# Recurrence of an RWKV-7 layer: another order of the woven projections and another split of them between inverses and carries

## The chip, the cores and the metric

The kernel runs on one core of one Trainium2 chip. The metric is the device time of one execution in microseconds (us). Engines: PE (TensorE, matmul), with PEld for its weight loads; DVE (VectorE); ACT (ScalarE); POOL (GpSimd); SP, whose queue issues nearly all DMAs. Each engine works through its own instructions in the order in which they stand; semaphores make one engine wait for another.

## The reference, cut to what matters

One layer: 640 tokens (512 of a latent grid, 128 of a context) of width 1024 go through a norm, one wide projection, two branches (RWKV-7 recurrence in both directions, neighbourhood attention), gates, an output projection and a gated feed-forward network. Everything is float32.

```python
u_rw, u_na, gate_rw, gate_na = jnp.split(h @ p["w_in"], IN_SPLITS, axis=-1)
o_rw, s_new = _rwkv_branch(u_rw, s0, p["shift_mu"], ...)
...
merged = (jax.nn.sigmoid(gate_rw) * (o_rw @ p["w_o_rwkv"])
          + jax.nn.sigmoid(gate_na) * (o_na @ p["w_o_na"]))

def _rwkv_branch(u, s0, mu, ...):
    u = _centred_shift(u, mu)          # u + mu0 * (prev - u) + mu1 * (next - u)
    r, k, v, wd, ad, gd = jnp.split(u, RW_SPLITS, axis=-1)
    ...
def _wkv_step(s, inp):                 # 8 heads of 64, forward and backward
    sa = jnp.einsum("bhvk,bhk->bhv", s, a)
    s = s * w[:, :, None, :] + sa[..., None] * b[:, :, None, :] + v[..., None] * k[:, :, None, :]
    return s, jnp.einsum("bhvk,bhk->bhv", s, r)
```

## The kernel before

**Stages.** The eight heads of the recurrence are handled in four stages (ct = 0 to 3), two heads of 64 features in one tile of 128 partitions by 640 tokens. The tokens are cut into 20 lines of 64 (ten forward, ten backward). A stage has three parts:

- `main`: products of keys inside a line (L1118, into `Nt`).
- `inv`, the inverse of a triangular 64x64 matrix per line. A recursion over s = 1 to 30 runs on DVE alone (L1228, L1242/L1246, L1235); then DVE transposes the result (L1255, L1257), PE multiplies half blocks (L1266), ACT copies them (L1271), DVE copies other blocks (L1274), PE multiplies again (L1280), and ACT and DVE write `Rt` (L1285). Beside the recursion PE makes products whose results DVE masks (L1149, L1152).
- `carry`: eight steps along the lines, each a chain of three parts: PE L1314 and ACT L1317; PE L1341 and ACT L1347; PE L1354 and DVE L1366, whose result the next step's L1314 reads. L1326, L1332 and L1371 are further small matmuls of a step.

**What runs beside them.** During carry ct the next stage is prepared (`prep`, L592 to L689: small matmuls, ACT exponentials, DVE products), in portions that `beside` hands out by a budget of ACT and DVE time per entry. In the last step, `last()` emits what is left of it, makes sure that the next r and v are there, and emits four L1097 (`akr`) and two L1100 on DVE; the next stage's L1118 reads what L1097 writes. The end of the former stage (`out`, L1378 to L1413) runs beside the next inverse.

**The woven matmuls.** PE also has the wide input projection to do: units of 48 matmuls 128x128 on 320 tokens (L192), each for 128 output columns: l0 to l2, k0 to k3, r0 to r3, v0 to v3 for the recurrence, g0 to g15 for the gates; then the merges a0 to a7 and b0 to b7. The generator `stream` runs the units in the order of `PRM["order"]`. I call one such matmul a fill. A unit's weights are loaded two units ahead by SP and cast when the unit before it has run an eighth: ACT writes the high part `whi` (L170), DVE or POOL the rest `wlo` (L171), by the unit's letter in `PRM["wl"]` (d or p).

What follows a unit differs. k, r and v have ACT copies into `U` (L505, L510, L511) and the centred shift: ACT L516 and DVE L517 and L519, each twice, 128 and 512 tokens wide; the shift of a later k, r or v writes the tile that the stage then reads. A gate has an ACT tanh (L538) for each half and a store of it by SP. These followers are emitted a few fills later (`later`, `tick`); in a carry they are held back and take slots of `beside`.

**The plan.** How many fills stand where is written by hand. `weave` takes one entry of `PRM["plan"]` at each yield of a stage's part:

```python
for _ in (_ for g in ((0,), gen, (0,)) for _ in g):
    p = next(plan)
    for _ in range(p[0]):
        if not next(fill, False):
            break
    for o_, n in zip(others, p[1:]):
        if bud:
            if n:
                beside(o_, bud[n - 1])
```

The first number of an entry is the fills. `inv` has 37 entries: one before it, one after its start, thirty after s = 1 to 30, one after the two transposes have been emitted and before L1266 (entry 32), then four around L1266, L1280 and L1285. `carry` has 26: one before, three for each of eight steps, one behind. All of this stands in PE's queue in the order written; PE cannot pass an instruction that waits.

Some units must wait: k(c+1) until the preparation has read the last k, r(c+1) until the bonus of stage c is done, v(c+1) until inverse c is done. `need` runs the stream on when a unit must be finished.

Of the kernel before, what the change touches and what calls it, by code (L numbers as in the profile page):

```python
# [26 lines left out]
PRM = dict(
    order=("l0 l1 k0 r0 v0 l2 g0 g1 g2 k1 g3 r1 g4 g5 v1 g6 g7 k2 r2 g8 g9 v2 g10 g11 k3 r3 g12 g13 v3 g15 g14 a0 a1 a2 a3 a4 a5 a6 a7 "
     "b0 b1 b2 b4 b3 b5 b6 b7"),
    plan=(  # L30
        "22.0 0.0 2.0 4.0",
        ("0.0.0 2.0.0 2.0.1 10.0.0 2.0.0 2.0.1 2.0.1 2.0.1 2.0.1 2.0.1 10.0.0 2.0.0 2.0.0 10.0.0 2.0.0 2.0.0 "
         "2.0.0 10.0.0 2.0.0 2.0.0 2.0.0 2.0.0 2.0.0 2.0.0 2.0.0 2.0.0 2.0.0 2.0.0 2.0.0 2.0.0 5.0.0 24.0.0 "
         "20.0.0 10.0.0 8.0.0 8.0.0 0.0.0"),
        ("10.0 1.0 12.1 0.2 0.0 8.1 6.2 0.0 8.1 6.2 0.0 8.1 12.2 0.0 8.1 6.2 0.0 8.1 6.2 0.0 7.1 5.2 0.0 9.1 "
         "6.2 6.0"),
        "22.0 2.0 2.0 2.0",
        ("0.0.0 0.0.0 2.0.1 10.0.0 1.0.0 2.1.1 2.1.1 2.1.1 2.1.1 1.1.1 10.0.0 3.0.0 2.0.0 2.0.0 2.1.0 2.1.0 "
         "2.0.0 10.0.0 2.0.0 2.1.0 2.1.0 2.1.0 2.1.0 2.1.0 12.1.0 2.1.0 2.1.0 2.1.0 2.0.0 2.1.0 5.0.0 24.0.0 "
         "20.0.0 10.0.0 8.0.0 8.0.0 0.0.0"),  # L40
        ("10.0 0.0 8.1 6.2 0.0 8.1 6.2 0.0 8.1 6.2 0.0 8.1 6.2 0.0 8.1 6.2 0.0 7.1 6.2 0.0 8.1 6.2 0.0 8.1 "
         "6.2 6.0"),
        "22.0 2.0 0.0 5.0",
        ("0.0.0 10.0.0 2.0.1 10.0.0 2.0.0 2.1.1 2.1.1 2.1.2 2.1.1 2.1.0 10.0.0 2.0.0 2.0.0 2.0.0 2.1.0 2.1.0 "
         "2.0.0 10.0.0 2.0.0 2.1.0 2.1.0 3.1.0 4.1.0 2.1.0 2.1.0 2.1.0 2.1.0 4.1.0 2.1.0 2.0.0 5.0.0 24.0.0 "
         "18.0.0 8.0.0 9.0.0 8.0.0 0.0.0"),
        ("10.0 0.0 8.1 14.2 0.0 8.1 6.2 0.0 8.1 6.2 0.0 0.1 6.2 0.0 8.1 6.2 0.0 8.1 6.2 0.0 8.1 6.2 0.0 8.1 "
         "6.2 6.0"),
        "22.2 0.0 4.0 6.0",
        ("0.0.0 16.1.0 8.1.1 9.0.0 2.1.0 8.1.1 8.1.1 8.1.1 8.1.1 0.1.1 0.1.0 0.0.0 0.1.0 0.1.0 0.1.0 0.1.0 "  # L50
         "6.1.0 7.1.0 6.1.0 6.0.0 6.0.0 6.0.0 0.0.0 6.0.0 6.0.0 7.0.0 6.0.0 6.0.0 6.0.0 6.0.0 6.0.0 6.0.0 "
         "11.0.0 8.0.0 8.0.0 2.0.0 0.0.0"),
        ("10.0 0.0 8.1 6.2 0.0 8.1 4.2 0.0 8.1 6.2 0.0 8.1 6.2 0.0 8.1 6.2 0.0 8.1 6.2 0.0 8.1 6.2 0.0 8.1 "
         "14.2 6.0"),
        "2 0 6 6 6 4 4 5 2 0 5 1 1 0 0"),
    qp=((0, 0, 7, 6, 7), (2, 5, 4, 4, 3, 2, 5, 3, 1)), ada=2, pa=1, pd=0,
    lw=(0, 0, 0, 0, 0, 2, 2, 2, 2, 2, 2, 2, 2, 2, 2, 2),
# [1931 lines left out]
```

## Time and profile before

| | us |
|---|---|
| median of three runs | 1223.24 (1219.85 to 1223.52) |
| the profiled execution | 1220.16 |
| its span, first to last instruction | 1218.4 |
| recurrence in it: first L1118 to last matmul of carry 3 | 276.2 to 690.7 |
| first L1118 of stages 0 to 3 | 276.2, 376.2, 481.2, 587.8 |
| first L1266 of stages 0 to 3 | 316.1, 426.1, 528.9, 648.3 |
| first L1314 of stages 0 to 3 | 326.7, 436.5, 538.9, 655.4 |

In the rows of the profile, `fl<-h,whi` is a fill that reads `h` and `whi`; a number in brackets at the end of a timeline row is the idle time of that engine before it, and what ended it. Matmuls overlap, so the price of one is read from the distance of starts and not from its own length. The granted clock is a share of full speed.

### The profile page before, as it was taken

How to read it: one execution, taken by the hardware profiler on the slowest of the kernel's cores; microseconds unless marked ns; L12 is line 12 of the kernel's file. 1: busy time of each engine (PE TensorE's matmuls, PEld its weight loads, DVE VectorE, ACT ScalarE, POOL GpSimd, SP SyncE). 2: the span in 40 equal slices, each digit the busy share in tenths (PEclk: the TensorE clock that was granted, in tenths of full speed). 3: DMA queues.
4: the chain of work that ended last, by engine and by line, in shares of the span. 5: the costliest groups of instructions: out<-in, count | busy, mean ns of one | idle time of the engine just before them, and what ended most of it. 6: DMA issues, size and time to landing. Idle time of an engine off the chain costs nothing.

```text
span 1218.4 us, 26820 instructions
## 1 busy us (share of the span) xinstructions
PE 1141.9 (94%) x11160; PEld 1008.2 (83%) x11160; DVE 796.2 (65%) x1630; ACT 504.1 (41%) x1016; POOL 251.7 (21%) x273
## 2 busy tenths in 40 slices
...
GB/s 336 248 110 104 211 197 228 188 96 79 61 46 53 80 53 48 56 82 40 49 214 95 129 294 97 75 52 87 121 36 87 87 104 55 86 88 102 67 72 104
DMA packets 56577, 134.47 MB, mean 110 GB/s; under 512 B 7140, under 2 KB 22116, under 8 KB 56456
## 3 DMA queue, kind: packets, MB, share of 16 engines
...
q14 instruction: 33, 0.27, 0.1%
...
## 4 chain that ended last, share of the span: by engine, by line
PE 61%; DVE 15%; ACT 4%; issue 3%; DMA 2%; POOL 0%; SPq 0%; DVEq 0%; ACTq 0%; POOLq 0%
PE f L1708 20%; PE acc L279 16%; PE fl L192 10%; DVE pr L1242 2%; DVE RL L1246 2%; PE mm L192 2%; PE w L1314 1%; PE w L1354 1%; PE w L1341 1%; PE w L1326 1%; DVE RL L1235 1%; PE po L939 1%; DVE AG L1149 1%; DMA wst<-in_w_o_dram 1%; DVE wlo L171 1%
## 5 line engine op out<-in xcount | busy, mean ns | idle before, releaser
L192 PE MATMUL fl<-h,whi 128*128 128x320 f32 x704 | 173.6, 328 | 1.8 <-ACT U L505 0.9
L1708 PE MATMUL f<-t,whi 128*128 128x320 f32 x640 | 142.4, 311 | 0.0
L1708 PE MATMUL f<-b,whi 128*128 128x320 f32 x608 | 135.6, 310 | 2.1 <-ACT b L181 1.8
L279 PE MATMUL acc<-whi,u 128*128 128x512 f32 (+1 forms) x448 | 136.0, 385 | 0.0
L192 PEld LDWEIGHTS fl<-h,whi 128*128 128x128 f32 x704 | 123.7, 196 | 6.7 <-ACT U L505 1.2
L171 POOL TENSOR_TENSOR wlo<-wst,whi 128x1024 fp32r<-128x1024 f32 (+2 forms) x37 | 79.7, 2153 | 207.0 <-ACT whi L170 203.6
L192 PE MATMUL fl<-h,wlo 128*128 128x320 f32 x352 | 116.3, 330 | 1.4 <-POOL wlo L171 1.4
L170 ACT CAST whi<-wst 128x1024 fp32r<-128x1024 f32 (+2 forms) x86 | 81.8, 957 | 76.8 <-PE acc L279 30.4
L1708 PEld LDWEIGHTS f<-t,whi 128*128 128x128 f32 x640 | 108.0, 189 | 0.0
L1708 PEld LDWEIGHTS f<-b,whi 128*128 128x128 f32 x608 | 101.9, 188 | 3.3 <-ACT b L181 2.2
L1708 PE MATMUL f<-t,wlo 128*128 128x320 f32 x320 | 99.4, 311 | 0.0
L1763 POOL TENSOR_TENSOR ws<-wst 128x512 f32<-128x512 f32 x20 | 27.6, 1381 | 341.2 <-DVE wlo L1752 226.7
L279 PEld LDWEIGHTS acc<-whi,u 128*128 128x128 f32 x448 | 83.5, 188 | 16.6
L1708 PE MATMUL f<-b,wlo 128*128 128x320 f32 x304 | 94.3, 310 | 2.2 <-DVE wlo L1752 2.2
L1749 ACT CAST whi<-ws 128x1024 fp32r<-128x1024 f32 x40 | 42.0, 1051 | 108.6 <-PE f L1708 47.5
L279 PE MATMUL acc<-wlo,u 128*128 128x512 f32 (+1 forms) x224 | 86.3, 385 | 0.0
L171 DVE TENSOR_TENSOR wlo<-wst,whi 128x1024 fp32r<-128x1024 f32 (+1 forms) x49 | 60.1, 1234 | 35.7 <-ACT whi L170 34.9
L279 PE MATMUL acc<-whi,h 128*128 128x512 f32 x240 | 79.2, 404 | 0.3 <-DVE h L393 0.3
L192 PEld LDWEIGHTS fl<-h,wlo 128*128 128x128 f32 x352 | 69.1, 196 | 4.2 <-POOL wlo L171 1.7
L192 PE MATMUL mm<-h,whi 128*128 128x320 f32 x288 | 69.5, 327 | 2.5 <-ACT U L505 2.5
L1548 DVE SCALAR_TENSOR_TENSOR tt<-acc,G 128x512 f32<-128x512 f32 (+1 forms) x51 | 34.7, 681 | 50.6 <-PE acc L279 50.6
L192 PE MATMUL fl<-o,whi 128*128 128x320 f32 x224 | 57.2, 335 | 6.6 <-DMA o<-o_d 5.2
...
## 6 DMA issues: line engine op xcount, KB each, us to landing
...
```

Source lines behind the costliest of these rows:

```text
L170: act.copy(hi[:, :n], st[:, :n])
L171: (eng or dve).tensor_tensor(out=lo[:, :n], in0=st[:, :n], in1=hi[:, :n].bitcast(F32), op=ALU.subtract)
L192: pe.matmul(ps[:, :t1 - t0], w[:, a:a + 128], x[:, k0 + kt, t0:t1], start=n == 0, stop=n == 3 * nk - 1)
L279: pe.matmul(pss[i][:, a:b], lhs(x, kt, ts_), w[:, cs_], start=ki == 0 and n == 0, stop=ki == last and n == 2)
L939: pe.matmul(pso[64 * hd:64 * hd + 64, :128], vt[:, hc:hc + 64], blk[k][hd][:, c * 128:(c + 1) * 128], start=c == 0, stop=c == len(vts) - 1)
L1149: dve.tensor_tensor(out=AG[oth, ls, h, :], in0=sq(pg, n)[oth], in1=V(K[oth, :], [[0, n], [1, 64]], KO["strict"]), op=ALU.mult)
L1242: dve.tensor_tensor(out=prv, in0=V(RL[:, s + 1 + a, :], [[32, b - a], [0, s]], s), in1=V(RL[:, s, :], [[0, b - a], [1, s]]), op=ALU.mult)
L1246: dve.tensor_tensor(out=dst, in0=dst, in1=prv, op=ALU.add)
L1548: dve.scalar_tensor_tensor(out=tt, in0=ps[:, a:b], scalar=c, in1=G[:, g, sl], op0=ALU.mult, op1=ALU.mult)
L1708: pe.matmul(ps[:, :H2], w_[:, c_], x_[:, kt, :], start=first and kt + n == 0, stop=last and kt == 3 and n == 2, skip_group_check=more)
L1749: act.copy(r[0][:, :width], src())
L1763: eng_x(PRM["se"][i - 1]).tensor_tensor(out=o_, in0=x, in1=y, op=op)
```

## The change

Only numbers and letters of `PRM` change. No instruction of PE is added or removed, and the fills sum to 1364 before and after.

- **Plan.** In stages 0 to 2, the entries of s = 18 to 27 (in stages 1 and 2 of s = 18 to 26) get two fills more, and the entry after s = 30 gets 38 for 24. Most entries of the carries get two fills less, a few four.

| fills of the plan | inverse 0 | carry 0 | inverse 1 | carry 1 | inverse 2 | carry 2 | inverse 3 | carry 3 |
|---|---|---|---|---|---|---|---|---|
| before | 165 | 132 | 164 | 127 | 167 | 128 | 188 | 134 |
| after | 199 | 98 | 196 | 95 | 199 | 96 | 188 | 134 |

- **Order.** r1, r2, r3 move behind two or three gates, and k2 and k3 move ahead of one. Followed through the plan, this is where units and what follows them come to stand:

| | before | after |
|---|---|---|
| inverse 0, s = 18 to its end | r1, g4 | g4, g5, most of r1 |
| shift of r1 | after the transposes of inverse 0 | carry 0, steps 0 and 1 |
| shift of v1 | carry 0, step 6 | carry 0, step 5 |
| inverse 1 | g7, k2, r2, g8 | k2, g7, g8, g9, part of r2 |
| shift of r2 | after the transposes of inverse 1 | carry 1, step 2 |
| inverse 2 | g11, k3, r3, g12 | k3, g11, g12, g13, start of r3 |
| shift of r3 | after the transposes of inverse 2 | carry 2, steps 2 and 3 |
| v3 fills forced by `need` before stage 3 | 12 | 8 |

- **Casts.** `wlo` of k1, v1, g6, r2, v2, g10, v3 and g15 is made by DVE and not by POOL, that of a4 by POOL and not by DVE.

```diff
-    order=("l0 l1 k0 r0 v0 l2 g0 g1 g2 k1 g3 r1 g4 g5 v1 g6 g7 k2 r2 g8 g9 v2 g10 g11 k3 r3 g12 g13 v3 g15 g14 a0 a1 a2 a3 a4 a5 a6 a7 "
+    order=("l0 l1 k0 r0 v0 l2 g0 g1 g2 k1 g3 g4 g5 r1 v1 g6 k2 g7 g8 g9 r2 v2 g10 k3 g11 g12 g13 r3 v3 g15 g14 a0 a1 a2 a3 a4 a5 a6 a7 "
...
         "22.0 0.0 2.0 4.0",
-        ("0.0.0 2.0.0 2.0.1 10.0.0 2.0.0 2.0.1 2.0.1 2.0.1 2.0.1 2.0.1 10.0.0 2.0.0 2.0.0 10.0.0 2.0.0 2.0.0 "
-         "2.0.0 10.0.0 2.0.0 2.0.0 2.0.0 2.0.0 2.0.0 2.0.0 2.0.0 2.0.0 2.0.0 2.0.0 2.0.0 2.0.0 5.0.0 24.0.0 "
-         "20.0.0 10.0.0 8.0.0 8.0.0 0.0.0"),
-        ("10.0 1.0 12.1 0.2 0.0 8.1 6.2 0.0 8.1 6.2 0.0 8.1 12.2 0.0 8.1 6.2 0.0 8.1 6.2 0.0 7.1 5.2 0.0 9.1 "
-         "6.2 6.0"),
+        ("0.0.0 2.0.0 2.0.1 10.0.0 2.0.0 2.0.1 2.0.1 2.0.1 2.0.1 2.0.1 10.0.0 2.0.0 2.0.0 10.0.0 2.0.0 "
+         "2.0.0 2.0.0 10.0.0 2.0.0 4.0.0 4.0.0 4.0.0 4.0.0 4.0.0 4.0.0 4.0.0 4.0.0 4.0.0 4.0.0 2.0.0 "
+         "5.0.0 38.0.0 20.0.0 10.0.0 8.0.0 8.0.0 0.0.0"),
+        ("10.0 1.0 8.1 0.2 0.0 6.1 4.2 0.0 6.1 4.2 0.0 6.1 8.2 0.0 6.1 4.2 0.0 6.1 4.2 0.0 5.1 3.2 0.0 "
+         "7.1 4.2 6.0"),
...
-         "2.0.0 10.0.0 2.0.0 2.1.0 2.1.0 2.1.0 2.1.0 2.1.0 12.1.0 2.1.0 2.1.0 2.1.0 2.0.0 2.1.0 5.0.0 24.0.0 "
...
+         "2.1.0 2.0.0 10.0.0 2.0.0 4.1.0 4.1.0 4.1.0 4.1.0 4.1.0 14.1.0 4.1.0 4.1.0 4.1.0 2.0.0 2.1.0 "
+         "5.0.0 38.0.0 20.0.0 10.0.0 8.0.0 8.0.0 0.0.0"),
...
-    wl="dddddddddppppppppppppppppppppppppppdpppppppppppp", nu=9, na=(
+    wl="ddddddddddppppddppppdddpppppddppppppppppppppppp", nu=9, na=(
```

Stage 3's entries are the same, only wrapped differently.

More of the change, by code (lines that the diff above doesn't have):

```diff
@@ L31 @@
         "22.0 0.0 2.0 4.0",
-        ("0.0.0 2.0.0 2.0.1 10.0.0 2.0.0 2.0.1 2.0.1 2.0.1 2.0.1 2.0.1 10.0.0 2.0.0 2.0.0 10.0.0 2.0.0 2.0.0 "
-         "2.0.0 10.0.0 2.0.0 2.0.0 2.0.0 2.0.0 2.0.0 2.0.0 2.0.0 2.0.0 2.0.0 2.0.0 2.0.0 2.0.0 5.0.0 24.0.0 "
-         "20.0.0 10.0.0 8.0.0 8.0.0 0.0.0"),
-        ("10.0 1.0 12.1 0.2 0.0 8.1 6.2 0.0 8.1 6.2 0.0 8.1 12.2 0.0 8.1 6.2 0.0 8.1 6.2 0.0 7.1 5.2 0.0 9.1 "
-         "6.2 6.0"),
-        "22.0 2.0 2.0 2.0",
-        ("0.0.0 0.0.0 2.0.1 10.0.0 1.0.0 2.1.1 2.1.1 2.1.1 2.1.1 1.1.1 10.0.0 3.0.0 2.0.0 2.0.0 2.1.0 2.1.0 "
-         "2.0.0 10.0.0 2.0.0 2.1.0 2.1.0 2.1.0 2.1.0 2.1.0 12.1.0 2.1.0 2.1.0 2.1.0 2.0.0 2.1.0 5.0.0 24.0.0 "
-         "20.0.0 10.0.0 8.0.0 8.0.0 0.0.0"),
@@ L41 @@
-        ("10.0 0.0 8.1 6.2 0.0 8.1 6.2 0.0 8.1 6.2 0.0 8.1 6.2 0.0 8.1 6.2 0.0 7.1 6.2 0.0 8.1 6.2 0.0 8.1 "
-         "6.2 6.0"),
-        "22.0 2.0 0.0 5.0",
[L44 to L48, printed above, removed]
@@ L49 @@
-        "22.2 0.0 4.0 6.0",
[L50 to L54, printed above, removed]
+        ("0.0.0 2.0.0 2.0.1 10.0.0 2.0.0 2.0.1 2.0.1 2.0.1 2.0.1 2.0.1 10.0.0 2.0.0 2.0.0 10.0.0 2.0.0 "
+         "2.0.0 2.0.0 10.0.0 2.0.0 4.0.0 4.0.0 4.0.0 4.0.0 4.0.0 4.0.0 4.0.0 4.0.0 4.0.0 4.0.0 2.0.0 "
+         "5.0.0 38.0.0 20.0.0 10.0.0 8.0.0 8.0.0 0.0.0"),
```

16 lines of the change are left out of this document (added).

## The prediction

> **What bounds the kernel now.** I read the page's head first, for the engine that is busy and the engine that ends the chain.
>
> ```profile
> span 1218.4 us, 26820 instructions
> PE 1141.9 (94%) x11160; PEld 1008.2 (83%) x11160; DVE 796.2 (65%) x1630; ACT 504.1 (41%) x1016; POOL 251.7 (21%) x273
> PE 61%; DVE 15%; ACT 4%; issue 3%; DMA 2%; POOL 0%; SPq 0%; DVEq 0%; ACTq 0%; POOLq 0%
> ```
>
> TensorE is busy 94%, but the share is an average. So I cut the recurrence by stage: from the first half-product of an inverse (L1266) to the first carry matmul (L1314), which I call the tail, and from there to the next stage's L1118 (in stage 3 to the last carry matmul), which I call the carry. Columns: length, busy time and instructions of PE, PEld, DVE, ACT, POOL, then the granted clock.
>
> ```profile
> core 0: us, PE busy (x) PEld busy (x) DVE busy (x) ACT busy (x) POOL busy (x), PEclk, DMA share, GB/s
> 316.11:326.73 10.62, 10.62 (x196) 9.94 (x197) 7.25 (x15) 3.79 (x9) 0.48 (x1) 0.69 0.07 24
> 326.73:376.15 49.42, 47.63 (x624) 41.93 (x623) 25.21 (x41) 26.82 (x71) 10.81 (x11) 0.97 0.17 55
> 426.10:436.47 10.37, 10.37 (x197) 9.83 (x197) 7.36 (x15) 3.36 (x8) 1.32 (x2) 0.71 0.11 40
> 436.47:481.18 44.71, 44.70 (x619) 39.81 (x618) 22.65 (x38) 25.78 (x70) 12.35 (x12) 1.00 0.16 51
> 528.92:538.94 10.02, 10.02 (x195) 9.48 (x195) 9.18 (x13) 5.47 (x12) 4.48 (x4) 0.73 0.23 69
> 538.94:587.84 48.90, 48.09 (x637) 42.49 (x636) 23.21 (x42) 26.86 (x73) 10.28 (x11) 1.00 0.18 57
> 648.25:655.41 7.16, 7.16 (x189) 6.64 (x189) 6.63 (x14) 2.40 (x6) 0.82 (x1) 1.00 0.28 78
> ```
>
> In the carries of stages 0 to 2 PE works almost without a gap (47.63 of 49.42, 44.70 of 44.71, 48.09 of 48.90), with DVE and ACT about half busy. The tails are PE-busy too, but at 0.69 to 0.73 of the clock; stage 3's runs at 1.00. The waits of PE tell why; the rows are the ends of the inverses of stages 1, 2 and 3, a wait for weights in stage 1, and one wait in carry 0.
>
> ```profile
> PE w L1266 <- DVE f L1255: 2.6, 1, 2.6
> PE fl L192 <- POOL wlo L171: 1.4, 1, 1.4
> ...
> PE w L1266 <- DVE f L1255: 3.7, 1, 3.7
> ...
> PE w L1266 <- DVE f L1255: 0.2, 1, 0.2
> ...
> PE w L1314 <- DVE ZV L1366: 1.5, 1, 1.5
> ```
>
> The timeline has stage 0's wait, and the price of a woven matmul ("fill") before and after it:
>
> ```profile
> 309.02 0.46 PE L192 MATMUL fl<-h,whi 128*128 128x320 f32 x2
> ...
> 309.46 0.46 PE L192 MATMUL fl<-h,whi 128*128 128x320 f32 x2
> ...
> 316.11 1.48 PE L1266 MATMUL w<-f,Nt 32*32 32x32 f32 x80 [4.87 <-DVE f L1255]
> ...
> 318.75 0.73 PE L192 MATMUL fl<-h,whi 128*128 128x320 f32 x2
> ...
> 319.55 0.73 PE L192 MATMUL fl<-h,whi 128*128 128x320 f32 x2
> ```
>
> Three fills go by in 0.44 us (0.147 each) before the wait, in 0.80 (0.267) after it. So DVE bounds an inverse's end, PE idles there 4.9, 2.6 and 3.7 us and restarts at half clock, and PE bounds the carry.
>
> **Term 1, carries.** The plan's sums fall from 132, 127, 128 fills to 98, 95, 96 in stages 0 to 2: 98 fewer, 98 x 0.147 = 14.4 us less PE work. Does the chain behind them allow it? A step without other work, from stage 3:
>
> ```profile
> 676.08 0.54 ACT L1347 COPY ZV<-w 64x128 f32<-64x128 f32 x2 [0.55 <-PE w L1341]
> ...
> 677.33 0.45 PE L1354 MATMUL w<-ZV,TG 128*64 128x64 f32 x8
> ...
> 677.83 0.61 DVE L1366 TENSOR_TENSOR ZV<-w,Dt 64x128 f32<-64x128 f32 x2 [0.25 <-PE w L1354]
> ...
> 679.02 0.45 PE L1314 MATMUL w<-ZV,AG 128*64 128x64 f32 x8
> ```
>
> ACT is done at 676.62 and PE comes 0.71 later; DVE at 678.44, PE 0.58 later. Two fills fewer at each place (0.29) still leave PE last. Four things give time back.
>
> (a) Twelve of the 98 stand behind a carry's last L1366. There DVE leads: it runs on from L1366 to the four L1097 that L1118 needs.
>
> ```profile
> 365.81 0.61 DVE L1366 TENSOR_TENSOR ZV<-w,Dt 64x128 f32<-64x128 f32 x2
> 366.45 2.22 DVE L680 TENSOR_TENSOR f<-NK,pre 128x640 f32<-128x640 f32 x1
> ...
> 371.48 0.82 DVE L680 TENSOR_TENSOR f<-NK,pre 128x640 f32<-128x640 f32 x1
> ...
> 372.94 3.37 DVE L1097 TENSOR_TENSOR AG<-kk,P 64x640 f32<-64x640 f32 x4
> ```
>
> That ends at 376.31, and L1118 starts at 376.15. 12 x 0.147 = 1.8 us gain nothing.
>
> (b) r1, r2 and r3 were projected by an inverse's end; their shifts (four DVE operations, ACT copies ahead of them) ran in the tails. Now they fall into carry steps between L1347 and L1366. The row of v1's shift is the price: two of its operations
>
> ```profile
> 364.25 0.75 DVE L517 SCALAR_TENSOR_TENSOR vp<-U,C,vp 128x512 f32<-128x512 f32 x1
> 365.03 0.75 DVE L519 SCALAR_TENSOR_TENSOR vp<-U,C,vp 128x512 f32<-128x512 f32 x1
> ```
>
> held L1366 until 365.81 and PE for 1.5 us. What is late is the next step's L1314, and all PE work queued behind it. Bounds 0 (the shift lies under PE work) and 2.1 (1.5 and the four fills taken out of that step) each; I take 1.5: 4.5 us.
>
> (c) After that wait the clock fell:
>
> ```profile
> 366.15:368.00 1.85, 1.85 (x25) 1.41 (x25) 1.82 (x2) 0.62 (x2) 1.84 (x1) 0.77 0.00 0
> 368.00:370.00 2.00, 2.00 (x8) 2.00 (x9) 1.50 (x3) 1.24 (x3) 0.00 (x0) 0.50 0.51 133
> 370.00:372.00 2.00, 2.00 (x18) 1.60 (x17) 2.00 (x3) 1.40 (x4) 0.00 (x0) 0.85 0.44 173
> ```
>
> 0.23 x 1.85 + 0.50 x 2 + 0.15 x 2 = 1.7 us of PE lost. Three new waits could cost 0 to 5.2; stage 1's wait of 2.6 lowered the clock as well, so I take one of three, as they are shorter: 1.7. [...]
>
> (d) Shifts take slots from the preparation of the next stage: two of its 0.82 us operations come to stand behind the last L1366 in stages 0 and 1, one fewer in stage 2. In stage 0 POOL's cast, which stretched L680 to 2.22, comes earlier (-1.4). 1.6 - 1.4 + 1.6 - 0.8 = 1.0.
>
> Carries: -14.4 + 1.8 + 4.5 + 1.7 + 1.0 = -5.4 (from -14.4 to -0.1, with 6.3 and 5.2 for b and c).
>
> **Term 2, inverses up to L1266.** They get 34, 32 and 32 fills: 5.0, 4.7, 4.7 us. Against idle of 4.87 stage 0 ends 0.1 later. Stage 1 has 2.6, and the 1.4 and more that its fills waited for weights and U tiles: about even. In stage 2 PE alone would come 4.7 - 3.7 = 1.0 late. But DVE's own chain moves as well, by the casts, since gates now follow each other faster there:
>
> ```profile
> 312.86 1.16 DVE L1235 SCALAR_TENSOR_TENSOR RL<-RL 128x28 f32<-128x28 f32 x6
> ...
> 418.76 2.40 POOL L171 TENSOR_TENSOR wlo<-wst,whi 128x1024 fp32r<-128x1024 f32 x1
> ...
> 418.87 5.25 DVE L1235 SCALAR_TENSOR_TENSOR RL<-RL 128x28 f32<-128x28 f32 x6
> ...
> 512.52 1.89 DVE L1242 TENSOR_TENSOR pr<-RL 128x114 f32<-128x114 f32 x2
> ```
>
> The six L1235 take 1.16 us alone and 5.25 under two POOL casts: 2.0 each. In stage 2 a cast that POOL had to wait for costs 1.89 less some 0.46, 1.4. Stage 1 loses the two behind L1235 (-4.1), gets g9's earlier (+1.4 to 2.0) and r2's on DVE itself (+1.2):
>
> ```profile
> L171 DVE TENSOR_TENSOR wlo<-wst,whi 128x1024 fp32r<-128x1024 f32 (+1 forms) x49 | 60.1, 1234 | 35.7 <-ACT whi L170 34.9
> ```
>
> -1.2. Stage 2 gets g13's and r3's ahead of the transposes, 2 x 1.4 to 2 x 2.0: 3.5. Stage 0 keeps two. Sum: 0.1 - 1.2 + 3.5 = +2.4, between -1.2 (r3's cast falls beside the transposes, and PE is on time) and +5.
> [...]
> The other casts given to DVE (k1, v1, g6, v2, g10, v3, g15) lie where DVE is half busy; cover gone, 1.2 each.
>
> **Term 3, tails.** Stage 3's tail holds 28 fills in 7.16 us at full clock; stage 0's and 1's 36, stage 2's 35. At full clock: 7.16 + 8 x 0.147 = 8.34, 8.34, 8.19, that is -2.3, -2.0, -1.8 if PE does not idle at L1266. I take stage 0 whole, stage 1 half (DVE and PE arrive within 1 to 2 us), stage 2 nothing (DVE late by 2.5). -3.3; bounds -6.1 and 0.
>
> **Term 4, the rest.** Four of v3's matmuls fewer are forced before stage 3 (8 for 12) and come out behind the last carry: +0.6. a4's half-size cast goes from DVE to POOL in stage 3's inverse: half of 1.2 saved, at most half of 2.0 blocked, taken as 0. A gate issues two stores on SP that wait for its tanh, with the load for the unit after next behind them; one unit of 48 fills (7 us) covers that load, so 0.
>
> Sum: -5.4 + 2.4 - 3.3 + 0.6 = -5.7 on the profiled execution's 1220.16 us. The median of the runs is 1223.24, 3.1 above it; I carry the difference over: 1217.5.
>
> **Rivals.** *PE bounds everything.* Nothing stalls: -14.4, tails -6.1, inverses +1.1, +0.6: -18.8, 1204.4. For it: PE 44.70 of 44.71 in carry 1. Against: the row of v1's shift. Chance 0.14.
> *The vector engine's ring.* From L1366 through preparation, L1097 and the recursion to L1255 DVE does the same work wherever fills stand, and sets the carries too: their gain is 0; -3.3 + 2.4 + 0.6 = -0.3, 1222.9. For it: 365.81 to 376.31 without a gap. Against: DVE 22.65 busy of 44.71. Chance 0.21.
> *Slower: the clock.* With fewer fills in a carry every wait of 1.5 us there buys a half-clock window of 1.7. Two more in each of three carries: +10.2 - 5.7 = +4.5, 1227.7. It decides from the fourth further window on (3 x 1.7 = 5.1). For it: the 0.50 row. Against: carries 1 and 2 at 1.00 now. Chance 0.27.
>
> **How the numbers follow.** The forecast has 0.38, with its own range 1212 to 1220. 0.3% is 3.7 us, about what a measurement of this kernel can tell. Faster: 0.38 + 0.14 = 0.52; within: 0.21; slower: 0.27. The range, 1206 to 1229, leaves out most of the first rival and a clock that falls oftener than eight times in all.
>
> **What would show it.** Right: L1266 without a wait and the clock at 1.00 behind it in stage 0; clean carry steps of 3.7 us in place of 4.3 (679.02 less 0.59); L1314 waiting for L1366 where r's shift lies; L1235 short in stage 1 and long in stage 2. Wrong: carries of unchanged length with DVE busy throughout, or 0.50 in the middle of carries.

## The result, and the profile after

The changed kernel takes 1230.36 us (median of four runs, 1228.76 to 1231.55) where the kernel before took 1222.78 in the same comparison: a ratio of 1.0064, 95% interval 1.005 to 1.0078. It is slower by some 7.6 us; 1217.5 had been forecast. A second comparison gave 1.0052 (1.0027 to 1.0077).

The head of the page of after:

```profile
PE 1145.4 (93%) x11160; PEld 1008.4 (82%) x11160; DVE 802.9 (65%) x1637; ACT 504.1 (41%) x1016; POOL 226.7 (18%) x266
...
PE 65%; DVE 13%; ACT 4%; issue 2%; DMA 1%; SPq 0%; POOL 0%; DVEq 0%; ACTq 0%; POOLq 0%
```

It hardly differs from before's, and so does not tell where the time went. The cut by stage does. The rows are after's tails of stages 0 to 2, its carries 0 to 2, and its inverses of stages 2 and 3 up to L1266 (columns as in the prediction):

```profile
316.49:324.81 8.32, 8.32 (x197) 7.80 (x197) 6.40 (x12) 3.28 (x9) 1.00 (x2) 1.00 0.26 85
424.94:433.27 8.33, 8.33 (x197) 7.80 (x197) 6.71 (x12) 4.41 (x9) 1.32 (x2) 1.00 0.36 120
535.21:543.39 8.18, 8.18 (x195) 7.66 (x195) 6.17 (x12) 4.19 (x9) 0.13 (x1) 1.00 0.20 75
...
324.81:373.73 48.92, 43.72 (x590) 37.89 (x589) 26.94 (x46) 26.64 (x72) 5.18 (x10) 0.93 0.11 36
433.27:479.91 46.64, 42.21 (x588) 36.62 (x587) 25.77 (x43) 25.47 (x71) 7.85 (x12) 0.96 0.13 42
543.39:591.90 48.51, 45.63 (x600) 39.80 (x600) 25.64 (x45) 27.51 (x75) 7.00 (x10) 0.93 0.12 36
...
479.91:535.21 55.30, 47.43 (x848) 42.84 (x849) 48.40 (x141) 20.54 (x41) 15.41 (x15) 0.94 0.19 64
591.90:657.05 65.15, 50.52 (x843) 43.59 (x844) 44.49 (x148) 15.64 (x32) 15.38 (x15) 0.92 0.40 134
```

The same two inverses before:

```profile
481.18:528.92 47.74, 40.46 (x818) 36.74 (x817) 42.77 (x141) 18.89 (x38) 14.65 (x16) 0.99 0.17 60
587.84:648.25 60.41, 48.54 (x844) 43.78 (x844) 42.50 (x147) 17.26 (x35) 13.24 (x15) 0.92 0.43 145
```

The tails came down to 8.32, 8.33 and 8.18 at full clock: 6.2 us gained. The carries, with 98 fills fewer, changed by -0.5, +1.9 and -0.4: PE was idle there 2.6 us in all before (lengths less PE busy) and 12.5 after, and the clock stands at 0.93 to 0.96. The inverses grew by 0.3, 1.3, 7.6 and 4.7. Together: -6.2 + 1.0 + 13.9, and 1.6 behind the last carry: 10.3 of the 10.4 us between the two spans (1228.8 and 1218.4).

*Carry 0.* The timeline has DVE and POOL of after around its longest wait, the waits view what PE paid:

```profile
354.91 0.74 DVE L517 SCALAR_TENSOR_TENSOR vp<-U,C,vp 128x512 f32<-128x512 f32 x1
355.69 2.91 DVE L519 SCALAR_TENSOR_TENSOR vp<-U,C,vp 128x512 f32<-128x512 f32 x1
358.63 0.61 DVE L1366 TENSOR_TENSOR ZV<-w,Dt 64x128 f32<-64x128 f32 x2
...
355.71 2.34 POOL L171 TENSOR_TENSOR wlo<-wst,whi 128x1024 fp32r<-128x1024 f32 x1 [16.50 <-ACT whi L170]
```

```profile
PE w L1314 <- DVE ZV L1366: 4.0, 1, 4.0
```

L519 took 0.75 before. Now a cast of POOL starts 0.02 us behind it and L519 takes 2.91; L1366 stands behind it, and PE waits 4.0. The 2.16 us more are nearly the cast's whole 2.34, and over the 1.4 that I had mixed in. By the rows DVE starts first, by 0.02 us, and is the one that is held.

*Inverse 2.* The groups of DVE in that stretch, before and then after (columns: count | busy us, mean ns | idle):

```profile
L1242 DVE TENSOR_TENSOR pr<-RL 128x110 f32<-128x110 f32 (+22 forms) x48 | 11.7, 283 | 0.0
L1246 DVE TENSOR_TENSOR RL<-RL,pr 128x110 f32<-128x110 f32 (+22 forms) x48 | 10.7, 263 | 0.0
...
L1235 DVE SCALAR_TENSOR_TENSOR RL<-RL 128x28 f32<-128x28 f32 (+2 forms) x6 | 1.1, 238 | 0.0
```

```profile
L1246 DVE TENSOR_TENSOR RL<-RL,pr 128x110 f32<-128x110 f32 (+22 forms) x48 | 12.9, 308 | 0.0
L1242 DVE TENSOR_TENSOR pr<-RL 128x110 f32<-128x110 f32 (+22 forms) x48 | 12.4, 297 | 0.0
...
L1235 DVE SCALAR_TENSOR_TENSOR RL<-RL 128x28 f32<-128x28 f32 (+2 forms) x6 | 3.2, 596 | 0.0
```

As many instructions, and 2.2, 0.7 and 2.1 us more. The timeline of after shows why: two casts of POOL (g13's and r3's) and the two operations of DVE that they stretch.

```profile
526.43 2.41 POOL L171 TENSOR_TENSOR wlo<-wst,whi 128x1024 fp32r<-128x1024 f32 x1 [0.44 <-ACT whi L170]
530.74 2.41 POOL L171 TENSOR_TENSOR wlo<-wst,whi 128x1024 fp32r<-128x1024 f32 x1 [1.89 <-ACT whi L170]
...
526.33 2.62 DVE L1246 TENSOR_TENSOR RL<-RL,pr 128x75 f32<-128x75 f32 x2
...
529.91 3.29 DVE L1235 SCALAR_TENSOR_TENSOR RL<-RL 128x28 f32<-128x28 f32 x6
```

*Inverse 3.* The loads of `o` (L1426) overwrite the buffers of `h`, so they wait for the last fill of g14 (SP's L1426 for L192: 8.1 us before, 5.9 after). These fills in the inverse, with first and last start; before, then after:

```profile
L192 PE MATMUL fl<-h,wlo x18: 307/309/552, 592.2 to 606.8; 128*128 128x320 f32 x18
```

```profile
L192 PE MATMUL fl<-h,wlo x20: 302/309/415, 596.2 to 612.1; 128*128 128x320 f32 x20
```

SP's timeline has the loads; before, then after:

```profile
606.69 7.10 SPq L1426 DMA_DIRECT2D o<-o_d  x12
```

```profile
612.29 7.35 SPq L1426 DMA_DIRECT2D o<-o_d  x12
```

And the windows show the 8 us in which PE restarts on them; before, then after:

```profile
612.00:616.00 4.00, 3.48 (x13) 3.18 (x14) 0.13 (x1) 0.00 (x0) 0.00 (x0) 0.50 1.02 399
616.00:620.00 4.00, 3.99 (x28) 3.14 (x30) 4.00 (x16) 0.92 (x1) 0.00 (x0) 0.96 1.00 387
```

```profile
616.00:620.00 4.00, 3.05 (x11) 2.30 (x11) 1.51 (x6) 0.92 (x1) 0.00 (x0) 0.57 0.99 333
620.00:624.00 4.00, 3.66 (x9) 2.17 (x8) 0.00 (x0) 0.00 (x0) 0.00 (x0) 0.50 1.03 404
```

The load goes out 20.4 us behind the stage's start instead of 18.9. PE's first fill that reads `o` is no later for that (24.4 us behind the stage's start, 24.7 before). But half clock lasts through the second 4 us as well (0.50 for 0.96), with L1071 and L1086 of the inverse in PE's queue between those fills.

### The profile page after: what moved, and what is told of

Read it like the earlier page. It is cut to its first block, busy times and chain, and to the rows that moved or that the text cites. A ratio compares the mean times of both kernels' runs of the same rounds, so it can differ in the third digit from the quotient of the medians.

```text
span 1228.8 us, 26813 instructions
## 1 busy us (share of the span) xinstructions
PE 1145.4 (93%) x11160; PEld 1008.4 (82%) x11160; DVE 802.9 (65%) x1637; ACT 504.1 (41%) x1016; POOL 226.7 (18%) x266
## 4 chain that ended last, share of the span: by engine, by line
PE 65%; DVE 13%; ACT 4%; issue 2%; DMA 1%; SPq 0%; POOL 0%; DVEq 0%; ACTq 0%; POOLq 0%
PE f L1708 21%; PE acc L279 16%; PE fl L192 12%; PE mm L192 2%; DVE RL L1246 2%; DVE pr L1242 2%; PE w L1314 1%; PE w L1354 1%; PE w L1326 1%; PE w L1341 1%; DVE AG L1097 1%; PE po L939 1%; ACT L L905 1%; PE w L1140 1%; PE w L1332 1%
## 5 line engine op out<-in xcount | busy, mean ns | idle before, releaser
L192 PE MATMUL fl<-h,whi 128*128 128x320 f32 x704 | 171.1, 324 | 3.7 <-ACT fl L538 3.7
L192 PEld LDWEIGHTS fl<-h,whi 128*128 128x128 f32 x704 | 120.1, 191 | 9.1 <-ACT fl L538 4.2
L192 PE MATMUL fl<-h,wlo 128*128 128x320 f32 x352 | 113.3, 322 | 0.0
L171 DVE TENSOR_TENSOR wlo<-wst,whi 128x1024 fp32r<-128x1024 f32 x56 | 69.3, 1243 | 38.3 <-ACT whi L170 37.3
L171 POOL TENSOR_TENSOR wlo<-wst,whi 128x1024 fp32r<-128x1024 f32 (+2 forms) x30 | 56.3, 1878 | 161.5 <-ACT whi L170 161.5
L192 PE MATMUL mm<-h,whi 128*128 128x320 f32 x288 | 69.7, 327 | 2.2 <-ACT U L505 2.2
L192 PEld LDWEIGHTS fl<-h,wlo 128*128 128x128 f32 x352 | 67.1, 191 | 2.5 <-issue 0.2
L192 PE MATMUL fl<-o,whi 128*128 128x320 f32 x224 | 57.2, 335 | 9.6 <-DMA o<-o_d 4.8
```

The costliest lines, as they stand in the source:

```text
L171: (eng or dve).tensor_tensor(out=lo[:, :n], in0=st[:, :n], in1=hi[:, :n].bitcast(F32), op=ALU.subtract)
L192: pe.matmul(ps[:, :t1 - t0], w[:, a:a + 128], x[:, k0 + kt, t0:t1], start=n == 0, stop=n == 3 * nk - 1)
```

## The experiments

All lengths in us, from one profiled execution each: inverse from a stage's first L1118 to its first L1266, tail to its first L1314, carry to the next stage's L1118 (carry 3 is 35.3 to its last matmul in all of them). Times are medians, ratios against the runs of before beside them. Those had medians of 1222.78 (after), 1219.84 (e1 to e4), 1221.32 (e5 to e8), 1219.47 (e9, e10) and 1222.40 (e11), so kernels of different groups are compared by their ratios.

| kernel | inverses 0 to 3 | tails 0 to 3 | carries 0 to 2 | time | ratio, 95% |
|---|---|---|---|---|---|
| before | 39.9 50.0 47.7 60.4 | 10.6 10.4 10.0 7.2 | 49.4 44.7 48.9 | 1222.78 | |
| after | 40.2 51.2 55.3 65.2 | 8.3 8.3 8.2 7.2 | 48.9 46.6 48.5 | 1230.36 | 1.0064 (1.005 to 1.0078) |
| e1_plan | 42.1 52.6 56.2 64.9 | 9.8 9.4 10.4 9.2 | 47.8 44.5 43.7 | 1232.94 | 1.0103 (1.0069 to 1.0136) |
| e2_order | 40.1 49.8 52.8 61.8 | 10.6 10.7 9.7 7.2 | 52.3 47.7 50.3 | 1234.76 | 1.0122 (1.0098 to 1.0146) |
| e3_casts | 40.2 51.4 53.0 64.3 | 8.3 8.3 8.2 9.2 | 48.9 46.7 46.8 | 1228.42 | 1.0067 (1.0039 to 1.0096) |
| e4_offset | 40.3 51.4 54.8 62.4 | 8.3 8.3 8.2 7.2 | 48.9 46.7 48.5 | 1226.34 | 1.004 (1.001 to 1.007) |
| e5_after_d | 42.1 54.2 51.4 59.5 | 8.3 8.3 8.2 7.2 | 45.0 44.5 46.3 | 1212.80 | 0.9941 (0.9922 to 0.996) |
| e6_before_d | 40.8 45.8 47.2 59.2 | 10.4 8.3 9.7 7.2 | 49.2 45.0 48.9 | 1214.86 | 0.9956 (0.9934 to 0.9977) |
| e7_dummy | 40.2 51.3 51.0 59.5 | 8.3 8.3 8.3 7.1 | 49.3 44.7 50.4 | 1220.48 | 0.9998 (0.9984 to 1.0012) |
| e8_warm | 40.1 50.8 54.8 63.5 | 8.3 8.3 8.2 8.7 | 47.2 45.2 46.6 | 1222.86 | 1.0007 (0.999 to 1.0024) |
| e9_mix | 42.1 46.4 47.0 60.3 | 8.3 9.6 10.0 7.2 | 45.0 44.7 48.9 | 1213.27 | 0.9944 (0.9924 to 0.9965) |
| e10_mixwarm | 43.6 46.7 47.0 56.2 | 8.3 9.9 8.3 7.2 | 46.0 44.7 49.5 | 1209.17 | 0.9914 (0.9886 to 0.9941) |
| e11_after_again | 40.2 50.8 55.7 64.6 | 8.3 8.3 8.2 8.7 | 48.9 45.2 46.5 | 1227.71 | 1.0052 (1.0027 to 1.0077) |
| e12_before_again | 40.0 49.5 47.9 60.1 | 9.7 10.1 9.7 7.1 | 49.2 44.7 48.9 | 1218.60 | one run |

### The change in two halves

e1_plan is before with after's `plan`; e2_order is before with after's `order` and `wl`:

```diff
--- before
+++ e1_plan
...
-        ("10.0 1.0 12.1 0.2 0.0 8.1 6.2 0.0 8.1 6.2 0.0 8.1 12.2 0.0 8.1 6.2 0.0 8.1 6.2 0.0 7.1 5.2 0.0 9.1 "
-         "6.2 6.0"),
+        ("10.0 1.0 8.1 0.2 0.0 6.1 4.2 0.0 6.1 4.2 0.0 6.1 8.2 0.0 6.1 4.2 0.0 6.1 4.2 0.0 5.1 3.2 0.0 "
+         "7.1 4.2 6.0"),
...
--- before
+++ e2_order
-    order=("l0 l1 k0 r0 v0 l2 g0 g1 g2 k1 g3 r1 g4 g5 v1 g6 g7 k2 r2 g8 g9 v2 g10 g11 k3 r3 g12 g13 v3 g15 g14 a0 a1 a2 a3 a4 a5 a6 a7 "
+    order=("l0 l1 k0 r0 v0 l2 g0 g1 g2 k1 g3 g4 g5 r1 v1 g6 k2 g7 g8 g9 r2 v2 g10 k3 g11 g12 g13 r3 v3 g15 g14 a0 a1 a2 a3 a4 a5 a6 a7 "
...
-    wl="dddddddddppppppppppppppppppppppppppdpppppppppppp", nu=9, na=(
+    wl="ddddddddddppppddppppdddpppppddppppppppppppppppp", nu=9, na=(
```

> The plan of after with the order of units and the cast engines of before: fills moved, r1 to r3 still projected by the inverses' ends. Theory U (the units' places cost the time: r's shifts in the carries, casts of g12, g13 and r3 in inverse 2): the tails keep their gain of 6.2 us, carries 0 to 2 come out 3 to 5 us shorter than before instead of 1.0 longer, inverse 2 ends at most 3 us later than before, and the time is 1217 to 1222. Theory F (fewer fills in a carry let its waits come bare, and the clock falls, wherever the units lie): carries as long as before (within 1 us in sum), time within 2 us of after's 1230.4. In both, inverse 3 stays some 3 to 5 us longer than before, since its first units stand four fills later as in after.

> The order and cast engines of after with the plan of before: units moved, no fill moved. Theory U: tails as before (10.6, 10.4, 10.0), with half clock in them; carries 0 to 2 longer than before by 4 to 5 us in sum, by r's shifts; the first fills of g14 stand where before has them, so inverse 3 takes before's 60.4 within 1.5. Time 1225 to 1231. Theory F: carries within 1 us of before, time within 3 us of before's 1222.8.

Each half alone is slower than before, by 1.0% and 1.2%. The interval of e2_order lies above both of after's, that of e1_plan overlaps with them. The carries of e1_plan, then those of e2_order:

```profile
328.74:376.50 47.76, 43.02 (x590) 37.42 (x589) 25.92 (x43) 25.89 (x69) 7.41 (x9) 0.93 0.12 40
438.48:482.95 44.47, 40.57 (x587) 35.24 (x586) 22.41 (x38) 24.21 (x68) 10.01 (x11) 1.00 0.17 57
549.48:593.20 43.72, 42.69 (x600) 37.14 (x599) 22.81 (x39) 25.07 (x70) 10.41 (x12) 1.00 0.15 47
```

```profile
328.53:380.86 52.33, 48.44 (x624) 42.77 (x623) 30.29 (x49) 28.26 (x74) 5.76 (x11) 0.93 0.14 46
441.26:488.96 47.70, 45.36 (x619) 40.03 (x619) 27.16 (x44) 26.99 (x73) 7.97 (x14) 1.00 0.17 50
551.47:601.73 50.26, 48.52 (x637) 42.65 (x636) 26.44 (x45) 28.96 (x78) 5.57 (x11) 1.00 0.13 42
```

Fills taken out shorten the carries by 7.1 us in sum; units moved in lengthen them by 7.3, with 3 to 5 us more of DVE in each. So far theory U. But its times (1217 to 1222, and 1225 to 1231) are at least 11 and 4 us off. In e1_plan inverses 0 to 2 grow by 2.2, 2.6 and 8.4 and the tails gain 1.4 instead of 6.2: with before's order every unit is done sooner, so the shifts of r1, r2 and r3 come ahead of the transposes (2.2 us in inverse 0), and casts of POOL stretch operations of DVE there (two L1242 by 2.2 each in inverse 1). Inverse 3 grows by 4.5, as both theories had it. In e2_order inverse 2 alone grows by 5.1; DVE has 46.2 us of work there for 42.8. Order and plan belong together. e2_order's inverse 3 is 61.8, as forecast.

### Two suspects in the inverses of stages 2 and 3

e3_casts gives the casts of g12, g13, r3 and a4 to DVE, e4_offset puts four fills back behind carry 2's last L1366:

```diff
--- after
+++ e3_casts
-    wl="ddddddddddppppddppppdddpppppddppppppppppppppppp", nu=9, na=(
+    wl="ddddddddddppppddppppdddppdddddpppppdppppppppppp", nu=9, na=(
--- after
+++ e4_offset
-        ("10.0 0.0 6.1 10.2 0.0 6.1 4.2 0.0 6.1 4.2 0.0 0.1 4.2 0.0 6.1 4.2 0.0 6.1 4.2 0.0 6.1 4.2 "
-         "0.0 6.1 4.2 6.0"),
+        ("10.0 0.0 6.1 10.2 0.0 6.1 4.2 0.0 6.1 4.2 0.0 0.1 4.2 0.0 6.1 4.2 0.0 6.1 4.2 0.0 6.1 4.2 0.0 "
+         "8.1 6.2 6.0"),
```

> After with the casts (wlo) of g12, g13, r3 and a4 on DVE in place of POOL. A cast on POOL stretched one of DVE's operations by 2.1 to 2.2 us in after's inverse 2, three times; DVE's own takes 1.2. Theory U: DVE's chain in inverse 2 is 3 x 0.9 to 3 x 1.0 shorter, inverse 2 goes from 55.3 to 52.5, inverse 3 gains up to 0.7, time 1227.0 to 1228.0. Rival (inverse 2 is long by its half clock at the start, 480 to 485, and by PE's wait of 2.4 for ACT; the casts lie beside that): inverse 2 at 54.5 or more, time 1229.5 to 1231.

> After with the last fills of carry 2 as before (8 and 6 in place of 6 and 4), so that stage 3's units stand where before has them. Theory O (the loads of o into h's buffers wait for the last fill of g14; four fills later they land later, PE waits for them bare and runs 10 us at half clock behind the wait): the first load of o is issued 0.6 to 1.2 us sooner after stage 3's first L1118, L1188's last group starts at 32 to 33.5 us after it instead of 35.2, inverse 3 comes to 61 to 63 from 65.15, time 1226.5 to 1229. Rival (inverse 3 is long by a4's cast on POOL and the clock alone): inverse 3 within 1 us of 65.15, time 1229.5 to 1231.

In e3_casts inverse 2 takes 53.0 (52.5 was expected), as DVE has 45.41 us of work there in place of 48.40:

```profile
478.50:531.52 53.02, 47.53 (x848) 43.11 (x848) 45.41 (x144) 20.64 (x41) 7.80 (x12) 0.94 0.20 66
```

So what theory U says of inverse 2 held, short of its size; after's inverse 2 is 55.3 and 55.7 in two executions. The time, 1.0067, can't be told from after's: tail 3 was 2.0 us longer in the profiled execution, and after's second one has 1.5 of that too, without the edit. e4_offset brings inverse 3 to 62.4 from 65.2 and 64.6; the time goes the same way, though the intervals overlap. Its load of `o` goes out 20.1 us behind the stage's start, only 0.3 sooner, as PE lost 2.3 us at L1140 there for a cause the profile calls "issue"; what shrank is the stretch at half clock, from 10.2 us to 6.9. Theory O's length came true, but not its mechanism: in e1_plan, too, the load goes out 18.9 us behind the stage's start, as in before, and inverse 3 still takes 64.9. What the traces share is PE's place at the end of it. Where stage 3's units stand four fills later (both executions of after, e1_plan, e3_casts, e8_warm), DVE is through with L1255 2.1 to 2.4 us before L1266 starts; in both executions of before, in e2_order, e4_offset and e5_after_d it is 0.2 or less. So the four fills cost 2.2 to 2.7 of the 4.7, by the order of fills and inverse in PE's queue and not by the load's start. The other half is open.

### All casts off POOL, in both kernels

e5_after_d is e4_offset, e6_before_d is before, both with one row of cast engines (the four letters p in its middle are a0 to a3):

```diff
--- e4_offset
+++ e5_after_d
-    wl="ddddddddddppppddppppdddpppppddppppppppppppppppp", nu=9, na=(
+    wl="dddddddddddddddddddddddddddddddppppdppppppppppp", nu=9, na=(
--- before
+++ e6_before_d
-    wl="dddddddddppppppppppppppppppppppppppdpppppppppppp", nu=9, na=(
+    wl="dddddddddddddddddddddddddddddddppppdpppppppppppp", nu=9, na=(
```

> After with the four fills of e4_offset put back and every weight cast from k1 to g14, and a4's, on DVE: no cast of POOL is left that can stretch an operation of DVE in stages 0 to 2. Theory P (POOL's casts on DVE's list, and the four fills, are what the change lost): DVE's busy time in the inverse of stage 2 falls from 48.4 to 44.5 or less, carry 0's wait for L1366 from 3.95 to 1.5 to 2.7, the wait for L1118 of stage 2 under 1; the stages 0 to 2 gain 2, 3 and 6 us, stage 3 gains 4.7, and the time is 1213 to 1219, below before. Rival W (the waits come from the shifts and the fills that were taken away, and DVE pays 1.2 for each cast it takes): 1223 to 1227.

> Before with every weight cast from k1 to g14 on DVE: the same cure without the change. By theory P before gains as well, since its rows have stretched operations too (two L1235 in inverse 1, one in stage 2's L1228, the L519 at the ends of carries 1 and 2): 12 places where 0.9 to 1.3 is won, about half of them on the path that sets the end: 1212 to 1218. By rival W 1222 to 1228, as 22 casts of 1.23 join DVE's list. The difference between this run and e5_after_d is what the moved fills and units are worth without the casts: theory P says after is ahead or even by up to 4 us; rival W says it stays 5 or more behind.

Both beat before, by 0.6% and 0.4%. The waits and the length of e5_after_d's carry 0:

```profile
PE w L1314 <- DVE ZV L1366: 2.0, 2, 1.8
```

```profile
325.27:370.21 44.94, 41.72 (x590) 36.07 (x589) 25.93 (x47) 26.74 (x72) 3.13 (x10) 1.00 0.12 39
```

The wait fell from 4.0 to 1.8, the clock stays at 1.00, and the carry is 4.0 us shorter. The time is 8.5 us under before's in the same comparison, and by the ratios 1.1 to 1.2% under after's. Taking the casts off POOL gains 1.0% in the changed kernel (from e4_offset, by the ratios) and 0.4% in the unchanged one. So what the change lost hangs on the casts' places and, in a smaller part, on the four fills, and not on the moved fills as such. Without both, changed and unchanged kernel stand at 0.9941 and 0.9956, which their intervals do not separate. By stages theory P was right for 0 (2.1 us shorter), 2 (6.1) and 3 (5.7), and wrong for stage 1, which came out 0.9 longer where 3 less were expected: its inverse takes 54.2. DVE's work in inverse 2 is 45.4 us, not 44.5 or less. In inverse 1 DVE waits 4.9 us at the shift of k2 (4.8 in after, below). The profiled execution was also 4 us above the kernel's median, so 54.2 may not be typical.

### The clock by itself

```diff
--- before
+++ e7_dummy
             phs = [wps(), wps()]
+            for _ in range((31, 16, 23, 0)[ct]):
+                pe.matmul(phs[0][:, :H2], hh[:, 0, :128], hh[:, 0, :H2], start=True, stop=True)
--- after
+++ e8_warm
                 px = wps()
+                for _ in range({(0, 6): 26, (1, 3): 11, (2, 4): 2}.get((ct, s), 0)):
+                    pe.matmul(px[:, :H2], hh[:, 0, :128], hh[:, 0, :H2], start=True, stop=True)
...
                 px = wps()
+                for _ in range(9 if (ct, s) == (2, 3) else 0):
+                    pe.matmul(px[:, :H2], hh[:, 0, :128], hh[:, 0, :H2], start=True, stop=True)
```

> Before with 31, 16 and 23 matmuls whose result is not used, of a fill's shape (128x128 by 128x320), placed ahead of L1266 in stages 0, 1 and 2: PE works through its wait for DVE, and no fill or unit moves. If the tails got shorter by the granted clock alone: tails 8.3, 8.3 and 8.2 in place of 10.6, 10.4 and 10.0, inverses and carries within 0.3 of before, and the time 5 to 6.5 us under before. Rival (the tails got shorter since r's shift left DVE's list there): tails shorter by under 1 us each, time within 3 us of before.

> After with matmuls of the same shape whose result is not used in three waits of the carries: 26 ahead of the L1314 of carry 0's seventh step (wait 3.95), 11 ahead of that of carry 1's fourth (1.67), 9 ahead of the L1341 of carry 2's fourth and 2 ahead of the next L1314. Theory K (half clock behind the waits is what ate the carries' gain): clock 1.00 through the carries, carries 0, 1 and 2 shorter by 2.4, 1.6 and 3 us, time 1222 to 1225. Theory W (the carry steps are held by ACT's and DVE's work, and a faster PE only waits longer for them): clock 1.00, carries shorter by under 1 us each, time 1228 to 1231.

Unused matmuls bring the whole gain of the tails, with r's shift where it was:

```profile
314.98:323.29 8.31, 8.31 (x197) 7.78 (x197) 7.37 (x15) 3.79 (x9) 0.49 (x1) 1.00 0.09 33
423.86:432.19 8.33, 8.33 (x196) 7.80 (x196) 7.37 (x15) 3.37 (x8) 1.32 (x2) 1.00 0.11 39
```

That gain is the clock alone. Yet the time did not move (0.9998): inverses 1 and 2 and carry 2 came out 1.3, 3.2 and 1.5 longer. Before's second execution, below, has its 49.5 and 47.9 again, which points at the unused matmuls. For inverse 2 the trace has the path. PE waits 2.9 us there at L1177 for a DVE operation of `out`, a wait that neither execution of before has, and runs at half clock behind it. It comes to the unused matmuls 47.5 us behind the stage's start; DVE is through at 48.1, but L1266 stands behind all 23 of them and starts at 51.0. Why L1177 waits, and what lengthened inverse 1 and carry 2, was not settled.

In e8_warm the clock is 1.00 in all three carries, and the time what theory K gave. But after, run once more without any edit, has carries 1 and 2 at 45.2 and 46.5 as well:

> After once more, for how far a stage's time repeats from one profiled execution to the next: if the stage times are the program's own, inverses 40.2, 51.2, 55.3 and 65.2, tails 8.3, 8.3, 8.2 and 7.2, carries 48.9, 46.6 and 48.5, each within 0.5. If inverse 2 or 3 differs by over 1.5, their part of the loss is put down with that much doubt.

> Before once more, for the same: inverses 39.9, 50.0, 47.7 and 60.4, tails 10.6, 10.4, 10.0 and 7.2, carries 49.4, 44.7 and 48.9, each within 0.5. If the inverses of stages 1 and 2 come out at 51.3 and 51.0 as in e7_dummy, the unused matmuls did not lengthen them.

```profile
323.20:372.14 48.94, 43.85 (x590) 38.00 (x589) 26.95 (x46) 26.66 (x72) 5.19 (x10) 0.93 0.11 36
431.28:476.46 45.18, 40.75 (x588) 35.36 (x587) 25.77 (x43) 25.52 (x71) 7.86 (x12) 1.00 0.13 42
540.36:586.81 46.45, 43.01 (x601) 37.40 (x600) 25.63 (x45) 27.46 (x75) 7.00 (x10) 1.00 0.12 38
```

The wait of PE in this carry 1, from the waits view of the same execution:

```profile
PE w L1314 <- DVE ZV L1366: 1.7, 1, 1.7
```

It is the same 1.7 us as in after's first profile, and the clock behind it there, from 451.40 on, was this:

```profile
451.40:454.00 2.60, 2.60 (x36) 2.28 (x37) 1.45 (x2) 1.10 (x4) 0.06 (x2) 0.76 0.07 14
454.00:456.00 2.00, 2.00 (x16) 1.67 (x17) 0.00 (x0) 1.55 (x5) 0.00 (x0) 0.50 0.73 250
```

In the second execution, where L1314 starts at 449.38, it stayed at 1.00:

```profile
449.40:452.00 2.60, 2.60 (x39) 2.33 (x40) 1.47 (x2) 1.18 (x4) 0.08 (x2) 1.00 0.11 20
452.00:456.00 4.00, 3.97 (x61) 3.28 (x59) 1.89 (x4) 3.07 (x9) 0.00 (x0) 1.00 0.34 124
```

So of e8_warm's shorter carries only carry 0's part (48.9 to 47.2) can be put down to the edit. The times say more: 1.0007 (0.999 to 1.0024) for e8_warm and 1.0052 (1.0027 to 1.0077) for after in its second comparison are some 5 us apart, and their intervals do not meet. The profiled execution of e8_warm was the slowest of its ten (1226.43). So keeping the clock in these three waits is worth some 5 us; where all but 1.7 of them lie was not shown. Before's stages repeat within 0.4, but for tail 0 (0.9 shorter); after's inverses 2 and 3 repeat within 0.6.

### The change where it paid

e9_mix is e6_before_d with after's plan in stage 0 alone and r1 behind g5; e10_mixwarm adds 18 unused matmuls ahead of stage 2's L1266.

```diff
--- e6_before_d
+++ e9_mix
-    order=("l0 l1 k0 r0 v0 l2 g0 g1 g2 k1 g3 r1 g4 g5 v1 g6 g7 k2 r2 g8 g9 v2 g10 g11 k3 r3 g12 g13 v3 g15 g14 a0 a1 a2 a3 a4 a5 a6 a7 "
+    order=("l0 l1 k0 r0 v0 l2 g0 g1 g2 k1 g3 g4 g5 r1 v1 g6 g7 k2 r2 g8 g9 v2 g10 g11 k3 r3 g12 g13 v3 g15 g14 a0 a1 a2 a3 a4 a5 a6 a7 "
...
--- e9_mix
+++ e10_mixwarm
             phs = [wps(), wps()]
+            for _ in range(18 if ct == 2 else 0):
+                pe.matmul(phs[0][:, :H2], hh[:, 0, :128], hh[:, 0, :H2], start=True, stop=True)
```

> The change in stage 0 alone, with the casts on DVE: the plan's stage 0 and the place of r1 from after, the stages 1 to 3 as before, every weight cast from k1 to g14 on DVE. If stages add up (stage 0 of e5_after_d 95.4 us from its first L1118 to the next stage's, of e6_before_d 100.3; stages 1 and 2 of e6_before_d 99.1 and 105.9, where e5_after_d has 107.1 and 105.9): 4.9 us under e6_before_d's 1214.9, 1208.5 to 1211.5, the fastest so far. Rival (what stage 0 gains comes back in stage 1, whose first units then stand elsewhere): 1213 to 1216.

> e9_mix with 18 matmuls of a fill's shape whose result is not used ahead of stage 2's L1266. If they only keep the clock: tail 2 from 9.7 to 8.2 to 8.4, everything else as in e9_mix, 1.4 us faster than it. Rival (in e7_dummy, which had 23 there and 16 in stage 1, inverses 1 and 2 came out 1.3 and 3.2 us longer; if the unused matmuls did that by delaying L1266): inverse 2 over 1.5 longer than e9_mix's and the time not under e9_mix's.

Stage 0 of e9_mix takes 95.4 us, as added up (97.9 in e10_mixwarm, with the same instructions up to there), but stage 1 gives 1.6 of it back, and 1213.27 is on the rival's side; its 0.9944 can't be told from e6_before_d's 0.9956. e10_mixwarm is the fastest here: 0.9914 (0.9886 to 0.9941), 10 us under before, and by the ratios 1.4 to 1.5% under after. Every run of it lies below every run of e9_mix; the medians are 4.1 us apart where 1.4 were expected. Tail 2 is 1.6 shorter, as expected. In the two profiled executions, 2.4 us apart, inverse 3 is also 4.1 shorter (56.2 for 60.3), and stage 0 is 2.5 longer. In inverse 3 PE waited 1.8 and 1.1 us for "issue" in e9_mix and not in e10_mixwarm; why was not tried.

## Why the prediction was wrong

The forecast was -5.7 us, and the profiled execution came out 10.4 longer by its span. Against their terms the tails were 2.9 better, the carries 6.4 worse, the inverses up to L1266 6.8 worse and the rest 5.8 worse. Most of the signs named for a right forecast were there: no wait at stage 0's L1266 and the clock at 1.00 behind it, clean carry steps of 3.5 to 3.7 us, a wait of L1314 at r2's shift, L1235 short in stage 1 and long in stage 2. So the mechanisms were largely the right ones, and the sizes were not; two costs were not in the sum at all.

*Term 3, tails, -3.3: too small.* They gave 6.2, the upper bound. Stage 2's L1266 still waited 1.5 us for DVE, and the clock held at 1.00. The halving for stage 1 and the zero for stage 2 were not needed.

*Term 1, carries, -5.4: measured +1.0, and -2.3 between the second executions.* The 14.4 us of fills did go: 140.4 us of PE work before, less 14.4, is 126.0, and the second execution of after has 127.6. (c) is the 1.6 us above that, as forecast (1.7), but 5.6 in the first execution (131.6): its size is a matter of the execution. So was the row that it rested on: in before's second execution the same L1314 of carry 0 waits 1.5 us too, and the clock is 1.00 over the whole carry. The idle time grew by 9.9, for which (a), (b) and (d) had 7.3. Of the 12.5 us of it in after, 2.9 are waits of L1118 for L1097 ((a) and (d) had 2.8), 3.6 are waits at the shifts of r1, r2 and r3 (0.2, 1.7 and 1.7; (b) had 4.5), and 1.6 are waits of L1371 for ACT in the last steps. What was missed is that a shift in a carry step meets a cast of POOL: 4.0 instead of 1.5 at v1's shift in carry 0, and 1.8 with the cast on DVE. Moved units cost the carries 7.3 us (e2_order), of which (b), (c) and (d) had 7.2; that these agree is in part luck, as (c) shows. The fills' gain was 7.1 in e1_plan, where half clock and DVE took the rest.

*Term 2, inverses up to L1266, +2.4: measured +9.2.* This is the step that failed most. Stage 2 was put at +3.5 for two casts at 1.4 to 2.0; they cost 2.2 each, a third adds 0.7, and DVE had lost 1.5 before the first of them, in waits for ACT (L1123) and PE (L1086). In the second execution of after inverse 2 is as long (55.7), but DVE is through 2.1 us before L1266, and PE, with the clock at 0.91 there, comes last. So the casts set this end in one execution only; in the first PE was there 1.5 us before DVE. With no cast on POOL inverse 2 is still 51.4 with the change and 47.2 without. DVE comes last in both; with the change it has two more L1097 to do in the inverse (1.6 us) and one more cast of its own (1.2).

In stage 1 DVE got shorter (44.96 to 43.41 busy), as predicted, yet the inverse longer by 1.3, and DVE still ends it (L1266 waits 0.4 for L1255). The move of k2 ahead of g7 had no price in the sum. The shift of k2 now stands 23 us behind the stage's start in DVE's list and not 39, and there DVE waits for ACT's part of it:

```profile
396.96 0.35 DVE L517 SCALAR_TENSOR_TENSOR kt__620<-U,C,kt__620 128x128 f32<-128x128 f32 x1 [4.80 <-ACT kt__620 L516]
```

The two stretched L1235 are gone, as forecast; this wait, and a cast that now stretches an L1242 by 2.2, take that back.

*Term 4, the rest, +0.6: measured +4.7 in inverse 3 and 1.6 behind the last carry.* The four fills "come out behind the last carry" was the error. They come out in front of g14, so every unit of inverse 3 stands four fills later, and the inverse's own matmuls stand behind them; e4_offset gives 2.2 to 2.7 us back by this alone. The rest of the 4.7, and the 1.6 (1.0 between the second executions), are open.

*The rivals.* "PE bounds everything" fell with the wait of 4.0. "The vector engine's ring" had the right engine, but its sum left out the casts and stage 3. "Slower: the clock" named 1227.7, next to the measured time, by another sum. By the granted clocks (0.93, 0.96 and 0.93, and 0.97 in carry 0 before) half clock took, as an estimate, some 17 us of after's carries and 3 of before's in the first executions, which costs PE at most 7 us, where this rival has 10.2. In the second execution of after only carry 0 had it, and after was still slower by 0.5%. Over the whole span half clock did not even grow, by an estimate that takes the clock as 0.50 or 1.00 throughout: 2 x (1 - 0.974) x 1218.4 is 63 us before, 2 x (1 - 0.976) x 1228.8 is 59 after (51 and 49 in the second executions). It moved from the tails into the carries and inverse 2. But keeping the clock behind three waits gave some 5 us back (e8_warm), so this rival was right in part. Its cure and that of the casts overlap: the longest of the three waits is made by a cast. How the loss divides between the two was not settled.
